# One core's hybrid SSD and retention layer: SSD output projection in block products, later norm transposes, first inputs by another queue

## The chip, the cores and the metric

The kernel runs on one core of one Trainium2 chip, as one program. The metric is device time in microseconds (us): the median of three runs.

## The reference

One decoder layer on 512 tokens of width 1024, all in float32. The stages that matter here, in order:

```
proj = x @ w_in                        # z, x|B|C, dt, q, k, v, g
y_ssd = norm(ssd_scan(...) * silu(z)) * norm_w      # 512 x 1024
y_ret = silu(g) * groupnorm(retention(q, k, v))     # 512 x 1024
mix = concat([y_ssd, y_ret]) @ w_mix_out            # (512 x 2048) @ (2048 x 1024)
x = LN(alpha * x + mix)
x = LN(alpha * x + cross_attention(x, mem))         # km = mem @ w_k, vm = mem @ w_v
h = conv3(x @ w_up + b_up); a, u = split(h)         # 2 x 2752 columns
x = LN(alpha * x + (silu(a) * u) @ w_down)
```

## The kernel before

**Products in three matmuls.** Each float32 operand is split into a high part (`wh`, a rounded copy made by ScalarE) and a low part (`wl`, the difference, made by VectorE or, for a few groups, by POOL). A product is the sum of high x high, high x low and low x high, three matmuls with up to 512 columns (`mm3`).

**Weights come in a planned stream.** `W` holds a list of weight groups of 128 x 1024 in the order of use. SP loads a group to a raw buffer (3 of them, tag `raw`), ScalarE and VectorE split it into a pair `wh`, `wl` (a ring of 4 pairs). `W.get` hands out the next pair and starts the split of the third one after it, which can run once the pair four before is no longer read. Groups made with `pool=True` (the eight for the memory keys) have their low part made by POOL.

**Block products.** `seven` multiplies a 512-token, 1024-row operand by a 1024 x 1024 matrix with seven products of halves instead of eight. The left operand's four blocks and their sums are made by a `Sides` object (`ready` makes the four sums for a piece, `make` splits a block), the weights' quarters and their sums by `Quarters` (eight loads of 128 x 1024, then `sums` on VectorE, L184 to L191, and splits, L196 and L197). Each product takes 2 weight pairs of 12 matmuls, goes to two PSUM banks, and its two results are added into the accumulator `acc` as they are done (`acc_quarter`). Without `seven`, `tok` does the same by 8 groups of 24 matmuls. The tuple `SEVEN` says which of four projections use it; before, these are the value projection `v` and the two halves of `down`. The SSD output projection has the branch in its code, which is not taken.

**The order around the SSD projection.** Before it come the last part of the z projection and then the output projection of the retention half (8 groups of 24 matmuls). Woven into this, TensorE transposes the finished SSD tiles (`ssd_out`: token tiles 0 to 3, eight 128 x 128 transposes each). Then comes the SSD half. As each of the four token tiles of `acc` is done, `norm(0, t)` runs: statistics on VectorE, a reciprocal root in two tiny POOL operations, two VectorE passes over 1024 columns (L957 and L964 before, six lines later after). TensorE goes on with the memory keys (8 groups with 256 columns, `keys`), then the memory values. `first_norm` sets after how many steps of these (a quarter of a key group, 0.68 us) the transposes of a normed tile come (`norm_t`).

**The MLP.** `up` is a stream of 43 groups of 24 matmuls. The first `down` block products are mixed into it: `UP_MIX` gives the number of up groups after each of the seven products, in the stream of weights and in TensorE's order alike.

**The start.** The input is transposed in four pieces of 256 rows. For the first, weights and input are loaded and split in halves; the rest goes by whole tiles of 512 KB. All these loads are issued by SP.

The order of instructions on each engine comes from a scheduler that follows the program's order and its own estimates; the engines run their lists in order.

Of the kernel before, what the change touches and what calls it, by code (L numbers as in the profile page):

```python
# [16 lines left out]
NT = 4  # L17
# [14 lines left out]
RAW = 3  # L32
NS = 37

SEVEN = ('v', 'down')
V_MIX = (1, 1, 1, 1, 0, 0, 0)
RET_MIX = (1, 1, 1, 1, 0, 0, 0)
UP_MIX = ((2, 2, 2, 2, 2, 2, 2), (1, 1, 1, 1, 1, 1, 1))

AHEAD = 4  # L40

# [18 lines left out]
def tile_layer(ctx, tc, wst, wdt, xt, xn, memt, rows, small_row, par, cst, mdec, out):  # L60
    nc = tc.nc
# [21 lines left out]
    def big(shape, dt=F32):  # L83
        return act.tile(shape, dt, tag="s", name=nm("s"), bufs=NS)
# [8 lines left out]
    def f(t):  # L93
        return t.bitcast(F32)
# [20 lines left out]
    def pair():  # L115
        return (ring.tile([P, 1024], F32R, tag="wh", name=nm("wh")),
                ring.tile([P, 1024], F32R, tag="wl", name=nm("wl")))

    def raw_slot():
        return ring.tile([P, 1024], F32, tag="raw", name=nm("raw"), bufs=RAW)  # L120

    class Group:
# [13 lines left out]
        def split(self, parts=1, between=None):  # L136
            r = raw_slot()
            h, l = pair()
            for i in range(parts):
                c = slice(i * 1024 // parts, (i + 1) * 1024 // parts)  # L140
                nc.sync.dma_start(out=r[:, c], in_=wst[self.n][:, c])
                copy = nc.vector.tensor_copy if parts > 1 and i == 0 else nc.scalar.copy
                copy(out=h[:, c], in_=r[:, c])  # L143
                (gtt if self.pool else tt)(out=l[:, c], in0=r[:, c], in1=f(h[:, c]), op=sub)  # L144
                if between is not None:
                    between(i, copy)
            return h, l
# [75 lines left out]
    def groups(n, k, pool=False):  # L223
        return [Group(n + i, pool) for i in range(k)]

    def mixed(products, others, after):

        out, others = [], list(others)
        for p, n in zip(products, after):
            out += p  # L230
            out += others[:n]
            others = others[n:]
        return out + others

    plan = groups(0, 8)
    plan += mixed(Quarters(8).items(), groups(16, 4), V_MIX) + groups(20, 8) if "v" in SEVEN else groups(8, 20)
    plan += groups(28, 12)
    plan += mixed(Quarters(44).items(), groups(40, 4), RET_MIX) if "ret" in SEVEN else groups(40, 12)
    plan += [q for p in Quarters(52, 8, 3).items() for q in p] if "ssd" in SEVEN else groups(52, 8)
    plan += groups(60, 8, True) + groups(68, 24)  # L240
    plan += groups(92, 4, True)
    up, down = groups(96, 12) + groups(116, 16) + groups(140, 11), groups(151, 6)
    if "down" in SEVEN:
        plan += up[:14] + mixed(Quarters(108).items(), up[14:28], UP_MIX[0])
        plan += up[28:30] + mixed(Quarters(132).items(), up[30:37], UP_MIX[1]) + up[37:]
    else:
        plan += up[:12] + groups(108, 8) + up[12:28] + groups(132, 8) + up[28:]
    plan += down
    W = Stream(plan)
# [75 lines left out]
    def behind(products, others, after):  # L325
        for p, n in zip(products, after):
            yield from p
            for _ in range(n):
                yield from next(others)
# [65 lines left out]
    def drain(*gens):  # L395
        for g in gens:
            for _ in g:
                pass
# [22 lines left out]
    for j in range(4):  # L421
        rv = big([P, 2, T])
        xv = xt[j].rearrange("p (k t) -> p k t", k=2)
        h, l = xT[j]
        x_raw.append(rv)

        def load_x(i, copy=nc.scalar.copy, n=1):
            nc.sync.dma_start(out=rv[:, i:i + n], in_=xv[:, i:i + n])
            copy(out=h[:, i:i + n], in_=rv[:, i:i + n])
            tt(out=l[:, i:i + n], in0=rv[:, i:i + n], in1=f(h[:, i:i + n]), op=sub)  # L430

        if j == 0:
            W.push(2, load_x)
        else:
            load_x(0, n=2)
            W.push()
# [142 lines left out]
    def x_quarter(i, j):  # L579
        return lambda k, t: x_lhs(4 * j + k, 2 * i + t)  # L580
# [22 lines left out]
    def k_and_v():  # L603
        if "v" in SEVEN:
            x_side = Sides(x_raw, {"11": x_quarter(0, 0), "12": x_quarter(0, 1), "22": x_quarter(1, 1)})
            for p in range(4):
                x_side.ready(p)
        yield from tok(x_lhs, all8, NT, rotary(1))
        if "v" in SEVEN:
            yield from behind(seven(x_side, v_quarter), bc_tiles(), V_MIX)  # L610
        else:
            for n in range(2):
                yield from tok(x_lhs, all8, NT, v_done(n))
# [382 lines left out]
    for j in range(2):  # L996
# [3 lines left out]
        rv = r.rearrange("p (k m) -> p k m", k=4)  # L1000
# [34 lines left out]
    xT = new_x()  # L1035

    def first_norm():
        for t in range(NT):
            yield 8
            norm_t(t)  # L1040

    dense = seq(keys(), *[tok(m_lhs, all8, 2, v_mem(n)) for n in range(2)])
# [186 lines left out]
    if "down" in SEVEN:  # L1229
        drain(*islice(up, 14))  # L1230
        drain(behind(seven(hid_side[0], acc_quarter(ALPHA)), up, UP_MIX[0]))
        drain(*islice(up, 2))
        drain(behind(seven(hid_side[1], acc_quarter()), up, UP_MIX[1]))
        drain(*up)
# [9 lines left out]
    for t in range(NT):  # L1244
        parts = THIRDS if t == NT - 1 else HALVES
# [141 lines left out]
```

## Time and profile before

| | |
|---|---|
| median of three runs | 928.28 us (928.28 to 928.32) |
| profiled execution | 928.88 us, of which its span is 926.4 us |
| TensorE matmuls | 911.5 us busy, 98% of the span |
| VectorE | 648.4 us, 70% |
| ScalarE | 369.6 us, 40% |
| POOL | 147.2 us, 16% |
| granted TensorE clock | 0.997 of 2.4 GHz |

The span runs from the first to the last instruction. The busy time of matmuls is modelled, since they overlap: one lasts 0.39 us in the rows while the next begins after 0.23. So waits are read from the starts.

### The profile page before, as it was taken

To read this page: it belongs to the slowest core of one execution; us is meant where nothing else is said; L and a number is where in the kernel's file an instruction comes from. 1 tells how busy PE (TensorE), PEld (TensorE's weight loads), DVE (VectorE), ACT (ScalarE), POOL (GpSimd) and SP (SyncE) were. 2 spreads that over 40 slices of the span, in tenths; PEclk is the share of its full clock that TensorE was granted. 3 is DMA by queue.
4 is the path that set the end of the run, shared out by engine and by line. 5 is a ranking of instruction groups with operands and counts; after the bars stand their busy time and mean duration, and the time that the engine had idled before them with its cause. 6 is when DMAs were issued, how large, how long until landed. Compare 5 with 4: busy or idle time off the path is not lost.

```text
span 926.4 us, 11580 instructions
## 1 busy us (share of the span) xinstructions
PE 911.5 (98%) x4535; PEld 757.0 (82%) x4535; DVE 648.4 (70%) x963; ACT 369.6 (40%) x545; POOL 147.2 (16%) x151
## 2 busy tenths in 40 slices
PE   9999999999999999999999999999999999999996
PEld 6788888877778888898888888988887888888885
DVE  5889757897854453478545669666779776897578
ACT  4236534355434431325434413543344443445330
POOL 1332011032525510163000007000000000000003
PEclk9999999999999999999999999999999999999998
DMA  7343122222212263426521222423333223331302
GB/s 287 105 146 127 39 76 69 69 69 70 69 46 69 91 230 109 138 92 205 190 82 46 69 69 95 134 91 98 108 133 118 68 69 114 125 119 52 114 23 91
DMA packets 26981, 95.24 MB, mean 103 GB/s; under 512 B 3120, under 2 KB 3632, under 8 KB 26928
## 3 DMA queue, kind: packets, MB, share of 16 engines
q1 hardware_dynamic: 25056, 88.09, 28.3%
q0 software_dynamic: 1728, 6.29, 2.0%
q8 instruction: 35, 0.57, 0.3%
q14 instruction: 18, 0.15, 0.0%
q10 hardware_dynamic: 144, 0.13, 0.0%
HBM read 92.41 MB, written 2.10 MB: 102 GB/s over the span
## 4 chain that ended last, share of the span: by engine, by line
PE 90%; DVE 5%; issue 1%; POOL 1%; DMA 1%; ACT 1%; SPq 0%; POOLq 0%; DVEq 0%
PE b L108 88%; PE b L112 3%; DVE s L964 1%; DMA s<-in_xt 1%; DVE s L957 1%; DVE st L952 1%; POOL st L465 1%; DVE s L1138 0%; DVE s L261 0%; DVE s L893 0%; DVE wl L197 0%; POOL st L464 0%; POOL s L960 0%; DVE wl L144 0%; DVE t L1175 0%
## 5 line engine op out<-in xcount | busy, mean ns | idle before, releaser
L108 PE MATMUL b<-s,wh 128*128 128x512 f32 (+1 forms) x1328 | 382.0, 372 | 3.3 <-DVE s L261 3.3
L108 PE MATMUL b<-wh,s 128*128 128x512 f32 (+1 forms) x1144 | 361.8, 391 | 0.6 <-DVE s L430 0.5
L108 PEld LDWEIGHTS b<-s,wh 128*128 128x128 f32 x1328 | 238.8, 189 | 47.2 <-DVE s L261 4.1
L108 PEld LDWEIGHTS b<-wh,s 128*128 128x128 f32 x1144 | 214.3, 188 | 48.3 <-DVE s L430 1.6
L144 DVE TENSOR_TENSOR wl<-raw,wh 128x1024 fp32r<-128x1024 f32 (+1 forms) x122 | 151.8, 1247 | 133.6 <-ACT wh L143 132.7
L108 PE MATMUL b<-s,wl 128*128 128x512 f32 (+1 forms) x664 | 245.1, 369 | 0.0
L143 ACT CAST wh<-raw 128x1024 fp32r<-128x1024 f32 (+1 forms) x133 | 139.2, 1049 | 215.8 <-PE b L108 195.1
L108 PE MATMUL b<-wl,s 128*128 128x512 f32 (+1 forms) x572 | 222.1, 388 | 1.4 <-DVE wl L197 1.4
L108 PEld LDWEIGHTS b<-s,wl 128*128 128x128 f32 x664 | 125.1, 188 | 21.3
L108 PEld LDWEIGHTS b<-wl,s 128*128 128x128 f32 x572 | 107.6, 188 | 23.6 <-DVE wl L197 1.7
L1175 DVE SCALAR_TENSOR_TENSOR t<-b,pr,t 128x511 f32<-128x511 f32 x86 | 64.2, 747 | 7.4 <-ACT t L1173 6.3
L197 DVE TENSOR_TENSOR wl<-s,wh 128x1024 fp32r<-128x1024 f32 x36 | 44.7, 1252 | 19.6 <-ACT wh L196 19.6
L196 ACT CAST wh<-s 128x1024 fp32r<-128x1024 f32 x36 | 37.8, 1053 | 50.2 <-PE b L108 40.7
L260 ACT CAST s<-b 128x512 fp32r<-128x512 f32 (+1 forms) x64 | 29.1, 484 | 55.7 <-PE b L112 22.5
L1201 POOL MEMSET t<- 64x512 f32 x1 | 0.5, 520 | 312.4 <-ACT t L1185 312.4
L144 POOL TENSOR_TENSOR wl<-raw,wh 128x1024 fp32r<-128x1024 f32 x12 | 32.7, 2738 | 68.2 <-ACT wh L143 68.2
L261 DVE TENSOR_TENSOR s<-b,s 128x512 fp32r<-128x512 f32 (+1 forms) x64 | 33.4, 550 | 13.9 <-ACT s L260 13.7
L1173 ACT ACTIVATE t<-b,cw,pr 128x512 f32<-128x512 f32 x43 | 33.3, 774 | 22.3 <-PE b L108 22.3
L893 DVE TENSOR_TENSOR s<-s,b 128x512 f32<-128x512 f32 x36 | 23.7, 680 | 15.4 <-PE b L108 15.4
L464 POOL TENSOR_TENSOR st<-st,epst 128x1 f32<-128x1 f32 (+1 forms) x16 | 5.6, 348 | 158.2 <-DVE st L953 157.8
L108 PEld LDWEIGHTS b<-s,t 128*128 128x128 f32 (+1 forms) x240 | 26.8, 180 | 3.1 <-PE b L108 0.9
L351 ACT CAST s<-s 128x512 fp32r<-128x512 f32 x36 | 20.7, 617 | 17.6 <-DVE s L1194 17.6
(164 smaller groups left out, 797.7 us busy)
## 6 DMA issues: line engine op xcount, KB each, us to landing
raw<-in_wst SPq DMA_DIRECT2D x132, 512.0 KB, 3.4
s<-in_wst SPq DMA_DIRECT2D x24, 512.0 KB, 4.7
s<-in_rows POOLq DMA_DIRECT2D x7, 512.0 KB, 6.2
s<-in_xn POOLq DMA_DIRECT2D x4, 512.0 KB, 5.8
s<-in_xt SPq DMA_DIRECT2D x3, 512.0 KB, 7.5
out_y<-s SPq DMA_DIRECT2D x3, 512.0 KB, 2.6
raw<-in_memt SPq DMA_DIRECT2D x2, 512.0 KB, 3.5
raw<-in_wst SPq DMA_DIRECT2D x2, 256.0 KB, 3.7
```

The lines of the kernel that those rows point to most:

```text
L108: pin(nc.tensor.matmul(o, lhsT=lhsT, rhs=rhs, start=start, stop=stop, skip_group_check=more))
L112: pin(nc.tensor.transpose(o, i, ident[:p, :p]))
L143: copy(out=h[:, c], in_=r[:, c])
L144: (gtt if self.pool else tt)(out=l[:, c], in0=r[:, c], in1=f(h[:, c]), op=sub)
L196: nc.scalar.copy(out=h, in_=src)
L197: tt(out=l, in0=src, in1=f(h), op=sub)
L260: nc.scalar.copy(out=h, in_=src)
L261: tt(out=l, in0=src, in1=f(h), op=sub)
L351: nc.scalar.copy(out=h[:, c, :], in_=src)
L893: tt(out=a, in0=a, in1=b, op=add)
L1173: nc.scalar.activation(out=c, in_=u, func=AF.Identity, bias=cw[0][:, i:i + 1], scale=ffp[:, i, 2:3])
L1175: stt(out=c[:, d:], in0=u[:, :T - d], scalar=ffp[:, i, 2 - d:3 - d], in1=c[:, d:], op0=mult, op1=add)
```

## The change

Five edits. The SSD output projection takes the branch with seven block products, and its weights are loaded as eight quarters (issued up to 8 groups ahead of the ring, summed up to 3 ahead). One up group moves from behind the last to behind the second down product. The first half of the input is issued from ScalarE's queue. The second input piece and second weights are loaded and split in halves, all by ScalarE and VectorE as for later ones. The transposes of the first normed tiles come after 13, 10, 10 and 8 steps instead of 8 each.

```diff
-SEVEN = ('v', 'down')
+SEVEN = ('v', 'ssd', 'down')
...
-UP_MIX = ((2, 2, 2, 2, 2, 2, 2), (1, 1, 1, 1, 1, 1, 1))
+UP_MIX = ((2, 3, 2, 2, 2, 2, 1), (1, 1, 1, 1, 1, 1, 1))
...
-                copy = nc.vector.tensor_copy if parts > 1 and i == 0 else nc.scalar.copy
+                copy = nc.vector.tensor_copy if between is not None and i == 0 else nc.scalar.copy
...
         def load_x(i, copy=nc.scalar.copy, n=1):
-            nc.sync.dma_start(out=rv[:, i:i + n], in_=xv[:, i:i + n])
+            if j > 0 or i > 0:
+                nc.sync.dma_start(out=rv[:, i:i + n], in_=xv[:, i:i + n])
             copy(out=h[:, i:i + n], in_=rv[:, i:i + n])
             tt(out=l[:, i:i + n], in0=rv[:, i:i + n], in1=f(h[:, i:i + n]), op=sub)

         if j == 0:
+            nc.scalar.dma_start(out=rv[:, 0:1], in_=xv[:, 0:1])
             W.push(2, load_x)
+        elif j == 1:
+            load_x(0)
+            W.push(2)
+            load_x(1)
         else:
...
     def first_norm():
-        for t in range(NT):
-            yield 8
+        for t, n in enumerate((13, 10, 10, 8)):
+            yield n
             norm_t(t)
```

VectorE before, at the end of the retention projection: the splits of plain weight groups and the four accumulations of its second half (L895).

```order
L144 TENSOR_TENSOR wl_2917<-raw_2915,wh_2916 128x1024
L144 TENSOR_TENSOR wl_2947<-raw_2945,wh_2946 128x1024
L144 TENSOR_TENSOR wl_2977<-raw_2975,wh_2976 128x1024
L895 SCALAR_TENSOR_TENSOR s_2681<-s_2681,b_2881 128x512
L895 SCALAR_TENSOR_TENSOR s_2682<-s_2682,b_2882 128x512
L895 SCALAR_TENSOR_TENSOR s_2683<-s_2683,b_2883 128x512
L895 SCALAR_TENSOR_TENSOR s_2684<-s_2684,b_2884 128x512
```

The same place after the change (L901 is the accumulation; 2908 and 2910 are the first quarters' two halves, 2912 is the second quarter's first half):

```order
L144 TENSOR_TENSOR wl_2926<-raw_2924,wh_2925 128x1024
L197 TENSOR_TENSOR wl_2955<-s_2908,wh_2954 128x1024
L184 TENSOR_TENSOR s_2908<-s_2916,s_2908 128x1024
L185 TENSOR_TENSOR s_2982<-s_2918,s_2908 128x1024
L197 TENSOR_TENSOR wl_2986<-s_2910,wh_2985 128x1024
L189 TENSOR_TENSOR s_2916<-s_2918,s_2916 128x1024
L184 TENSOR_TENSOR s_2910<-s_2920,s_2910 128x1024
L185 TENSOR_TENSOR s_3013<-s_2922,s_2910 128x1024
L189 TENSOR_TENSOR s_2920<-s_2922,s_2920 128x1024
L197 TENSOR_TENSOR wl_3017<-s_2912,wh_3016 128x1024
L901 SCALAR_TENSOR_TENSOR s_2687<-s_2687,b_2904 128x512
```

Six sums of weight quarters stand between the last weight splits and the last accumulations of the retention projection; the first of them needs the fifth of the eight loads.

POOL before, from the first key group on (L464 and L465 are a tile's reciprocal root):

```order
L144 TENSOR_TENSOR wl_3189<-raw_3187,wh_3188 128x1024
L144 TENSOR_TENSOR wl_3219<-raw_3217,wh_3218 128x1024
L144 TENSOR_TENSOR wl_3249<-raw_3247,wh_3248 128x1024
L464 TENSOR_TENSOR st_3262<-st_3261,epst 128x1
L465 TENSOR_TENSOR st_3262<-st_3262,mhalf 128x1
L464 TENSOR_TENSOR st_3279<-st_3278,epst 128x1
L465 TENSOR_TENSOR st_3279<-st_3279,mhalf 128x1
L144 TENSOR_TENSOR wl_3336<-raw_3334,wh_3335 128x1024
```

POOL after the change, the same place:

```order
L144 TENSOR_TENSOR wl_3292<-raw_3290,wh_3291 128x1024
L470 TENSOR_TENSOR st_3305<-st_3304,epst 128x1
L471 TENSOR_TENSOR st_3305<-st_3305,mhalf 128x1
L144 TENSOR_TENSOR wl_3332<-raw_3330,wh_3331 128x1024
L470 TENSOR_TENSOR st_3322<-st_3321,epst 128x1
L471 TENSOR_TENSOR st_3322<-st_3322,mhalf 128x1
L144 TENSOR_TENSOR wl_3350<-raw_3348,wh_3349 128x1024
L144 TENSOR_TENSOR wl_3403<-raw_3401,wh_3402 128x1024
```

The reciprocal roots of tiles 0 and 1 have moved ahead of the second and third key splits.

SP's first loads before the change (`raw` are weights, `s` the input):

```order
L141 DMA raw_94<-in_wst 128x512
L428 DMA s_93<-in_xt 128x512
L141 DMA raw_94<-in_wst 128x512
L428 DMA s_93<-in_xt 128x512
L141 DMA raw_113<-in_wst 128x1024
L428 DMA s_109<-in_xt 128x1024
L141 DMA raw_123<-in_wst 128x1024
```

And after it:

```order
L141 DMA raw_95<-in_wst 128x512 x2
L429 DMA s_93<-in_xt 128x512
L141 DMA raw_113<-in_wst 128x512 x2
L429 DMA s_109<-in_xt 128x512 x2
L141 DMA raw_129<-in_wst 128x1024
```

SP no longer issues the first half of the input, and the second weights and input have become two transfers each, the input's behind the weights'.

## Rows read from the trace of the kernel before

**Rows 1.** The page: TensorE's busy time, share of the span, instructions.

```profile
PE 911.5 (98%) x4535; PEld 757.0 (82%) x4535; DVE 648.4 (70%) x963; ACT 369.6 (40%) x545; POOL 147.2 (16%) x151
```

**Rows 2.** Chain of waits, 330 to 400: start, duration, what.

```profile
334.22 65.31 PE b L108 x288
```

**Rows 3.** VectorE's groups by shape: busy us, mean ns, idle before.

```profile
L197 DVE TENSOR_TENSOR wl<-s,wh 128x1024 fp32r<-128x1024 f32 x36 | 44.7, 1252 | 19.6 <-ACT wh L196 19.6
L352 DVE TENSOR_TENSOR s<-s,s 128x512 fp32r<-128x512 f32 x36 | 24.5, 703 | 2.2 <-ACT s L351 2.1
L893 DVE TENSOR_TENSOR s<-s,b 128x512 f32<-128x512 f32 x36 | 23.7, 680 | 15.4 <-PE b L108 15.4
...
L184 DVE TENSOR_TENSOR s<-s,s 128x1024 f32<-128x1024 f32 x6 | 7.3, 1223 | 0.1
```

**Rows 4.** VectorE's timeline, first down products: start, duration, count.

```profile
678.65 2.36 DVE L197 TENSOR_TENSOR wl<-s,wh 128x1024 fp32r<-128x1024 f32 x2
...
713.55 1.29 DVE L352 TENSOR_TENSOR s<-s,s 128x512 fp32r<-128x512 f32 x2
```

**Rows 5.** Stretches of two output projections: busy us of PE, PEld, DVE, ACT, POOL.

```profile
312.80:356.40 43.60, 43.60 (x210) 36.41 (x209) 20.72 (x26) 15.30 (x24) 11.41 (x21) 1.00 0.46 157
356.40:400.00 43.60, 43.60 (x194) 36.12 (x193) 15.59 (x19) 10.34 (x10) 5.45 (x3) 1.00 0.38 121
```

**Rows 6.** ScalarE's timeline: one of the casts, and its wait.

```profile
354.67 1.05 ACT L143 CAST wh<-raw 128x1024 fp32r<-128x1024 f32 x1 [4.38 <-PE b L108]
```

**Rows 7.** DMA issues: KB each, median us to landing.

```profile
s<-in_wst SPq DMA_DIRECT2D x24, 512.0 KB, 4.7
```

**Rows 8.** POOL's timeline, 388 to 426.

```profile
388.45 2.39 POOL L144 TENSOR_TENSOR wl<-raw,wh 128x1024 fp32r<-128x1024 f32 x1 [61.84 <-ACT wh L143]
...
402.07 0.56 POOL L465 TENSOR_TENSOR st<-st,mhalf 128x1 f32<-128x1 f32 x1
...
404.76 6.22 POOL L144 TENSOR_TENSOR wl<-raw,wh 128x1024 fp32r<-128x1024 f32 x2 [0.22 <-ACT wh L143]
...
420.42 5.72 POOL L144 TENSOR_TENSOR wl<-raw,wh 128x1024 fp32r<-128x1024 f32 x2
```

**Rows 9.** VectorE's timeline in the same stretch.

```profile
404.10 1.28 DVE L964 SCALAR_TENSOR_TENSOR s<-s,st,s 128x1024 f32<-128x1024 f32 x1
405.30 3.43 DVE L957 SCALAR_TENSOR_TENSOR s<-s,st,s 128x1024 f32<-128x1024 f32 x1
...
423.82 2.31 DVE L261 TENSOR_TENSOR s<-b,s 128x256 fp32r<-128x256 f32 x5
```

**Rows 10.** TensorE's timeline at the third set of transposes.

```profile
422.43 1.04 PE L112 MATMUL b<-cs,s 128*128 128x128 f32 x8
425.14 0.50 PE L108 MATMUL b<-s,wh 128*128 128x256 f32 x2 [1.68 <-DVE s L261]
```

**Rows 11.** TensorE's timeline in the third down product.

```profile
706.87 0.67 PE L108 MATMUL b<-wh,s 128*128 128x512 f32 x2
708.96 0.50 PE L108 MATMUL b<-wl,s 128*128 128x512 f32 x1 [1.41 <-DVE wl L197]
```

**Rows 12.** The start: SP, ScalarE, VectorE, TensorE in their timelines.

```profile
1.17 0.42 SPq L428 DMA_DIRECT2D s<-in_xt  x1
...
6.30 0.62 ACT L143 CAST wh<-raw 128x512 fp32r<-128x512 f32 x1 [4.29 <-DMA raw<-in_wst]
7.97 0.62 ACT L429 CAST s<-s 128x512 fp32r<-128x512 f32 x1 [1.05 <-DMA s<-in_xt]
9.32 1.05 ACT L143 CAST wh<-raw 128x1024 fp32r<-128x1024 f32 x1 [0.73 <-DMA raw<-in_wst]
10.56 1.06 ACT L429 CAST s<-s 128x1024 fp32r<-128x1024 f32 x1 [0.19 <-DMA s<-in_xt]
...
16.22 1.22 DVE L430 TENSOR_TENSOR s<-s,s 128x1024 fp32r<-128x1024 f32 x1
...
12.93 0.50 PE L108 MATMUL b<-wh,s 128*128 128x512 f32 x1 [0.51 <-DVE s L430]
```

## The prediction

> **What bounds the kernel now.** The page comes first [rows 1]: TensorE is busy for 98% of the span. So time is matmuls plus the few places where TensorE waits, and each edit is priced as matmuls removed plus waits removed, moved or made. The chain of waits gives the price of a matmul [rows 2]: 288 of them in 65.31 us, 0.2267 us each, across several changes of weights. Then I went through TensorE's timeline for starts further apart than that. From the output projections on there are three: in the memory keys at 423 us [rows 10], at the start of the MLP (the edit leaves it alone), and at 709 us inside the third block product of the first down projection [rows 11]. Others stand in the first 13 us [rows 12]. The tail behind the last matmul is untouched.
>
> **Part 1: 24 matmuls fewer.** The SSD projection goes from 2 x 8 x 4 x 3 = 192 matmuls to 7 x 2 x 2 x 2 x 3 = 168: 24 x 0.2267 = **-5.44 us**, if TensorE stays fed.
>
> *Is it fed?* VectorE gets most of the new work. By its durations [rows 3]: six more weight splits (14 pairs for 8) 6 x 1.25 = 7.5; eight sums of weight quarters, 8 x 1.22 = 9.8; eight sums of activation blocks of 512 columns, at the 0.70 of a split of that size, 5.6; 14 splits of these at 0.70, where there were 8 of transposes of the same size, 4.2; six more accumulations at 0.68, 4.1. Sum 31.2 us. The output projections of the two halves occupy 312.8 to 400, where VectorE is busy 20.7 and 15.6 us of 43.6 each [rows 5]. So 68 of some 82 us: possible if nothing stands late. VectorE is in order, so I follow its queue on the old time scale.
>
> The retention projection starts at 312.8; its eight weight pairs last 24 matmuls each (5.44), with four sets of transposes (0.87 each) between, so the SSD projection starts at S = 312.8 + 8 x 5.44 + 4 x 0.87 = 359.8, as now. Then a pair lasts 2.72, and E = S + 38.1 = 397.9 is its end. A pair is cast as soon as TensorE has left the pair four before: the casts start on that wait and take 1.05 [rows 6]. The eight quarter loads stand behind the two memory loads in SP's queue, and the second of these needs a raw buffer whose split can end at 334.1 (its ring place is left at 312.8 + 3 x 5.44 + 3 x 0.87 = 331.7; cast and split add 2.4). With 4.7 us for the first [rows 7] and 1.25 for each further one, the pace of whole loads in the first microseconds (9.32 to 10.56) [rows 12], all have landed by 349. VectorE's first sum of quarters can start at 345.8, behind the split of the first pair (343.5 + 2.3); the second pair's cast ends at 349.0 + 1.05. From there independent operations follow 1.14 us apart for 1024 columns and 0.60 for 512 (second starts inside 2.36 and 1.29 for two) [rows 4]. Counting on in the order shown: the fourth pair's low half is ready at 364.4, needed at S + 3 x 2.72 = 368.0; the sixth at 369.1, needed at 373.4; the last two at 386.7 and 389.3, needed at 392.5 and 395.2. Each product's accumulations end over 4 us before the next product but one takes their bank. I take **0** for this stage: a lead of 2.5 to 6 us covers it; without it each us is paid in full. Upper bound +4, with quarters landing 6 to 8 us later than I count.
>
> **Part 2: the memory keys and the later transposes.** The wait at 423 comes about so: the norm's last scalar-tensor-tensor stands against a POOL split of key weights (420.42 on) [rows 8], and lasts as long as the one begun at 405.30, 3.43 instead of 1.28 [rows 9]; behind it on VectorE stand the evictions that free the next PSUM bank (five from 423.82), and TensorE starts at 425.14 [rows 10]. Eight transposes take 0.87, so it lost 425.14 - 422.43 - 0.87 = 1.84 us. With the handover later (13, 10, 10, 8 steps) the evictions come before the bank is wanted.
>
> But another queue takes its place. POOL makes the low halves of the eight key pairs. Before, a pair of the projection lasted 24 matmuls, so POOL's first three splits ran before the norm, from 388.45 on. Now it lasts 12: the first can start at S + 11 x 2.72 + 1.05 = 390.8. POOL's order changes too, to one split and then the statistics of tile 0, where it was three. The rows show POOL's split and the norm's two long operations taking turns: alone 2.39 and 1.28 us, but the operation begun at 405.30 ends at 408.73, 1.09 after POOL's split (405.25 + 2.39), and POOL's second split ends at 404.76 + 6.22 = 410.98, 2.25 after that [rows 8, 9]. From 390.8 on: eight splits x 2.25 = 18.0; eight norm operations x 1.09 = 8.7; four reciprocal roots, each 0.56 for the power and about 0.2 for the sum, 3.0; about 0.9 of POOL waiting for a tile's statistics. Sum 421.4. TensorE wants the last at E + 7 x 2.72 + 2 x 0.87 = 418.7. That is 2.7 us of waiting for 1.84: **+0.9 us**. Bounds: -1.8 if POOL's splits go first throughout (390.8 + 18 + 3 = 411.8, in time), +4 if the evictions behind the norm hold a bank besides, as now.
>
> The Trainium skill's page "SBUF — State Buffer", section "Who interferes with whom", says that a VectorE instruction with two SBUF inputs and a GpSimd instruction that reads SBUF block each other entirely, whichever issues first. The rows of the norm agree (3.43 for 1.28). No row shows VectorE's weight split under a POOL split; by that rule the projection's last pair too would be held by up to 2.39, if VectorE came to it after 390.8. By my count it ends at 389.3.
>
> **Part 3: a third up group after the second down product.** The third product's second pair has its high weights at 706.87 (two matmuls, 0.45), and resumes with the low ones at 708.96 [rows 11]: 1.64 us lost to VectorE's split. The third group puts 5.44 us of matmuls ahead, so the low half is wanted 3 x 5.44 + 2.72 = 19.0 us after the second product's end. VectorE's list up to that split is nearly the same; its last wait is for the second group's bank (10.9 and 0.8 of ScalarE), then come two passes on that bank, two sums and the split, 4.9 us: 16.6 us, in time: **-1.64 us**. The group comes from behind the last product; the count before the next seven stays. Bounds 0 and -1.64.
>
> **Part 4: the first inputs.** ScalarE's casts start when a transfer lands: halves at 6.30 and 7.97, wholes at 9.32 and 10.56 [rows 12]. TensorE's matmul on the second input's low half waits until 12.93. An issue from ScalarE saves one of SP's, 0.42. Halving the second input and weights makes the last cast and split half as long (1.06 + 1.23 for the whole). Against this stand two more transfers, and here a half takes as long as a whole (1.67 between 6.30 and 7.97, 1.24 between 9.32 and 10.56). Gain bound: the third input's split ends at 17.44 as now, wanted at 12.93 + 24 x 0.2267 = 18.37: -0.9. Loss bound: two transfers x 1.24 later it ends at 19.9: +1.5. By bytes a half should cost half; the landings say more. I take a value between, **+0.3**.
>
> The skill's "DMA: Bandwidth & Descriptors", section "Issuing engines are not separate DMA queues", says that starting transfers on several engines saves the sequencer's issue time only. By it the first edit is worth at most that one issue.
>
> **Sum.** -5.44 + 0 + 0.9 - 1.64 + 0.3 = -5.9 us. The profiled execution took 928.88 (span 926.4), so 923.0; the runs' median, 928.28, is 0.6 lower: **922.4 us**.
>
> **Rivals.** *Keys without a wait* (POOL goes first, inputs gain 0.4): 928.28 - 5.44 - 1.84 - 1.64 - 0.4 = 919.0. For it: the handover now lies far behind the norm. Against: the turns in rows 8 and 9. Chance 0.20. *VectorE sets the pace in the projection*: about 3 us of waits from the third pair on, 925.4. For it the 68 of 82 us and the port rule; against it the lead counted above: 0.18. *All given back* (the same with the loss bounds of parts 2 and 4): 927 to 930: 0.08. *Slower*, by the quarter loads alone: they stand behind the memory loads, and VectorE stops at the first sum until its quarter lands, with all splits behind it. The last quarter is wanted at 353.7; beyond some 3.5 us of lead each us costs one. To end 1.9 us above the time before it must land near 365, sixteen after my count: 931. Against it, SP has nothing else to issue there: 0.06. My forecast, 921 to 925 by itself: 0.48.
>
> **Chances and range.** 0.2% (1.86 us) is about what a measurement can tell. Faster 0.86 (forecast 0.48, keys 0.20, VectorE 0.18), same 0.08, slower 0.06. The range 919.0 to 926.4 leaves out the lower half of the keys case and the last two.
>
> **What would show it.** Right: 168 matmuls in the projection at 0.2267 without a gap; POOL hardly idle from its first key split to its eighth, TensorE waiting on its low halves there; no wait in the third down product; the second input's matmuls under way between 12 and 13.5 us. Wrong: waits on quarter sums or weight splits in the projection; transposes waiting for their tile; the third input landing after 18 us.

## The result and the profile after

The changed kernel takes 924.01 us in the median of five runs (923.94 to 924.97); the kernel before, on the same chip, 928.32. The ratio is 0.995, with a 95% interval from 0.9937 to 0.9963: 4.3 us faster, where 5.9 were forecast. The sign and the range were right; two of the five terms of the sum were not, in opposite directions.

The profiled execution took 924.97 us, the slowest of the five; its span is 923.0 us, where the others have 922.1 to 922.2. The page's first part, to be held beside [rows 1]:

```profile
PE 908.1 (98%) x4511; PEld 755.4 (82%) x4511; DVE 680.0 (74%) x999; ACT 383.9 (42%) x575; POOL 149.4 (16%) x151
```

There are 24 matmuls fewer. 24 x 0.2267 is 5.44 us, but TensorE's busy time fell by 3.4 only. So either its matmuls got slower somewhere, or records hide a wait. Lines are six later than before. To find the place, I put the starts of the same matmuls of both traces side by side (behind the projection, the numbering is shifted by 24). The distance between them changes in four places and nowhere else:

| place | start before | start after | step |
|---|---|---|---|
| 60th matmul (counted from 0) | 18.73 | 17.48 | -1.25 |
| in the second key pair, behind the SSD projection | 407.15 | 400.45 | -5.45 |
| behind the keys | 453.89 | 451.86 | +4.67 |
| last matmul, behind the third down product | 918.35 | 914.55 | -1.77 |

The sum is -3.80. These are starts in one execution of each kernel, so a step holds to a few tenths of a us (how far for the first is shown with the two halves of the start edits). The last output lands 0.4 later in this one execution, so the span is 3.4 shorter.

**The projection.** The chain of waits after (start, duration, what), beside [rows 2], and VectorE's busy time (the third figure behind the length) in the same two stretches as [rows 5], the second cut off at the end of the projection:

```profile
332.97 55.79 PE b L108 x246
```

```profile
312.80:356.40 43.60, 43.60 (x210) 36.40 (x210) 29.56 (x35) 18.45 (x35) 10.40 (x18) 1.00 0.62 229
356.40:396.40 40.00, 40.00 (x178) 33.15 (x177) 39.22 (x51) 19.97 (x24) 6.35 (x5) 1.00 0.13 40
```

The reader is to see 55.79 / 246 = 0.2268 us per matmul, without a break, although VectorE is busy for 39.22 of 40.00 us in the second stretch. The last weight split, on VectorE:

```profile
387.19 1.23 DVE L197 TENSOR_TENSOR wl<-s,wh 128x1024 fp32r<-128x1024 f32 x1 [0.21 <-ACT wh L196]
```

It ends at 388.42. The forecast had 389.3 on the old time scale, 388.05 with the 1.25 us that the start gained.

**The memory keys.** TensorE's timeline after, where [rows 10] showed the wait before; in brackets the idle time and what ended it:

```profile
419.00 0.28 PE L108 MATMUL b<-s,wl 128*128 128x256 f32 x1
420.36 0.50 PE L108 MATMUL b<-s,wh 128*128 128x256 f32 x2 [1.07 <-ACT wh L143]
422.79 0.58 PE L108 MATMUL b<-s,wl 128*128 128x256 f32 x1 [1.93 <-POOL wl L144]
423.17 0.64 PE L108 MATMUL b<-s,wh 128*128 128x256 f32 x2
```

And the stretches of this stage (behind the length: busy time of PE, PEld, DVE, ACT, POOL, then the granted clock):

```profile
415.00:419.00 4.00, 3.88 (x33) 3.68 (x31) 3.52 (x4) 0.66 (x3) 1.35 (x1) 1.00 0.42 136
419.00:423.00 4.00, 0.99 (x6) 0.59 (x5) 2.35 (x3) 3.28 (x6) 2.62 (x2) 0.84 0.01 4
423.00:428.50 5.50, 5.50 (x24) 5.32 (x25) 4.87 (x8) 3.12 (x5) 0.81 (x2) 0.50 0.72 259
428.50:436.00 7.50, 7.50 (x38) 6.28 (x37) 3.56 (x7) 3.23 (x7) 0.00 (x0) 1.00 0.71 270
```

TensorE waits twice at the eighth key pair: first for ScalarE's cast, then for POOL's low half. From start to start these are 1.35 and 2.21 us where 0.12 is usual, so 3.3 us. And then the third row says "busy for 5.50 of 5.50" at a granted clock of 0.50, that is 1.2 GHz instead of 2.4: the matmuls begin 0.21 apart instead of 0.12. A busy share hides this; the clock column shows it. In the kernel before there was no such stretch.

This adds up to the step in the table. Held against one matmul each 0.12 us (256 columns) or 0.23 us (512), TensorE loses 3.3 us in the two waits, 2.7 in the slow stretch and 0.5 in three short waits just ahead; the bank wait of 1.84 is gone. 3.3 + 2.7 + 0.5 - 1.84 = 4.66.

What released each step is in the chain of waits after:

```profile
406.50 5.73 POOL wl L144 x2
412.24 1.13 POOL st L470
...
413.45 0.55 POOL st L471
...
414.03 3.40 DVE s L970
417.43 0.35 DVE s L261
...
417.80 0.38 ACT s L260
...
418.20 0.77 DVE s L261 x2
...
419.26 1.06 ACT wh L143
...
420.38 2.37 POOL wl L144
```

Read it upwards from the end. POOL's eighth split waits for ScalarE's cast of the eighth pair. This cast stands in ScalarE's list behind evictions (L260), these wait for VectorE's evictions (L261), these stand behind the second pass of the last tile's norm (L970), and this waits for the root (L471), which stands on POOL behind two key splits. POOL itself sat idle for 4.04 us ahead of its eighth split:

```profile
413.96 2.38 POOL L144 TENSOR_TENSOR wl<-raw,wh 128x1024 fp32r<-128x1024 f32 x1
420.38 2.36 POOL L144 TENSOR_TENSOR wl<-raw,wh 128x1024 fp32r<-128x1024 f32 x1 [4.04 <-ACT wh L143]
```

This trace also has a row of which the forecast found none, a weight split on VectorE beside a POOL split (the last one above). It takes 2.05 us, alone 1.22 (beside other work of POOL the kernel before has such a split of 2.59 us, at 205.72):

```profile
421.77 2.05 DVE L144 TENSOR_TENSOR wl<-raw,wh 128x1024 fp32r<-128x1024 f32 x1 [0.25 <-ACT wh L143]
```

**Start and third down product.** ScalarE's casts of the second input's second half and of the third input after, beside [rows 12]:

```profile
9.31 0.62 ACT L430 CAST s<-s 128x512 fp32r<-128x512 f32 x1 [0.19 <-DMA s<-in_xt]
...
13.14 1.05 ACT L430 CAST s<-s 128x1024 fp32r<-128x1024 f32 x1 [0.23 <-DMA s<-in_xt]
```

The third input is cast at 13.14, where the cast began at 15.13 before:

```profile
15.13 1.05 ACT L429 CAST s<-s 128x1024 fp32r<-128x1024 f32 x1 [0.17 <-DMA s<-in_xt]
```

No matmul of the second input waits. Of the wait at 709 us [rows 11] nothing is left. The chain of waits has one piece from the MLP's start to 898.4 us, where the last norms take over in the chain: 1464 matmuls, 0.218 us apart on average. The matmuls behind it, up to 914.55, have no gap either.

```profile
579.31 319.07 PE b L108 x1464
```

### The profile page after: what moved, and what is told of

It is laid out like the page before. It is cut to its first block, busy times and chain, and to the rows that moved or that the text cites. A ratio compares the mean times of both kernels' runs of the same rounds, so it can differ in the third digit from the quotient of the medians.

```text
span 923.0 us, 11614 instructions
## 1 busy us (share of the span) xinstructions
PE 908.1 (98%) x4511; PEld 755.4 (82%) x4511; DVE 680.0 (74%) x999; ACT 383.9 (42%) x575; POOL 149.4 (16%) x151
## 4 chain that ended last, share of the span: by engine, by line
PE 91%; POOL 3%; DVE 3%; issue 1%; ACT 1%; DMA 0%; POOLq 0%; DVEq 0%; ACTq 0%
PE b L108 88%; PE b L112 3%; POOL wl L144 2%; DVE s L970 1%; POOL st L470 1%; POOL st L471 1%; DVE st L958 1%; DMA raw<-in_wst 0%; DVE s L1144 0%; DVE s L261 0%; ACT wh L143 0%; DVE wl L144 0%; POOL s L966 0%; DVE s L963 0%; ACT s L965 0%
## 5 line engine op out<-in xcount | busy, mean ns | idle before, releaser
L108 PE MATMUL b<-wh,s 128*128 128x512 f32 (+1 forms) x1128 | 357.0, 391 | 0.1
L144 DVE TENSOR_TENSOR wl<-raw,wh 128x1024 fp32r<-128x1024 f32 (+1 forms) x115 | 142.9, 1245 | 109.1 <-ACT wh L143 108.6
L108 PE MATMUL b<-wl,s 128*128 128x512 f32 (+1 forms) x564 | 219.2, 389 | 0.0
L143 ACT CAST wh<-raw 128x1024 fp32r<-128x1024 f32 (+1 forms) x126 | 131.1, 1042 | 177.9 <-PE b L108 152.9
L196 ACT CAST wh<-s 128x1024 fp32r<-128x1024 f32 x50 | 52.5, 1053 | 77.9 <-PE b L108 59.7
L197 DVE TENSOR_TENSOR wl<-s,wh 128x1024 fp32r<-128x1024 f32 x50 | 61.6, 1242 | 21.8 <-ACT wh L196 21.8
L260 ACT CAST s<-b 128x256 fp32r<-128x256 f32 (+1 forms) x56 | 25.2, 464 | 55.7 <-DVE s L261 19.6
L261 DVE TENSOR_TENSOR s<-b,s 128x256 fp32r<-128x256 f32 (+1 forms) x56 | 28.8, 532 | 15.4 <-ACT s L260 15.0
L351 ACT CAST s<-s 128x512 fp32r<-128x512 f32 x50 | 28.8, 619 | 17.6 <-DVE s L1200 17.6
L352 DVE TENSOR_TENSOR s<-s,s 128x512 fp32r<-128x512 f32 x50 | 33.6, 696 | 3.0 <-ACT s L351 3.0
```

Of the source, the lines that this page charges most:

```text
L108: pin(nc.tensor.matmul(o, lhsT=lhsT, rhs=rhs, start=start, stop=stop, skip_group_check=more))
L196: nc.scalar.copy(out=h, in_=src)
L197: tt(out=l, in0=src, in1=f(h), op=sub)
L260: nc.scalar.copy(out=h, in_=src)
L261: tt(out=l, in0=src, in1=f(h), op=sub)
L351: nc.scalar.copy(out=h[:, c, :], in_=src)
```

## Experiments

The theory after the comparison: the loss is at the keys, made by POOL's splits and the norm in turn, by the cast that gets stuck behind them, and by the clock that falls behind the waits. The rivals: VectorE is simply too full there; the later handover is at fault; the clock falls for a reason of its own. First, the edits one at a time on the kernel before. "Last matmul" is the start of TensorE's last matmul in the profiled execution, 918.35 before.

**Start edits alone.**

```diff
-                copy = nc.vector.tensor_copy if parts > 1 and i == 0 else nc.scalar.copy
+                copy = nc.vector.tensor_copy if between is not None and i == 0 else nc.scalar.copy
...
-            nc.sync.dma_start(out=rv[:, i:i + n], in_=xv[:, i:i + n])
+            if j > 0 or i > 0:
+                nc.sync.dma_start(out=rv[:, i:i + n], in_=xv[:, i:i + n])
...
+            nc.scalar.dma_start(out=rv[:, 0:1], in_=xv[:, 0:1])
             W.push(2, load_x)
+        elif j == 1:
+            load_x(0)
+            W.push(2)
+            load_x(1)
```

> The kernel before with the edits of the start alone (first input half issued from ScalarE's queue; second input and second weights in halves). The forecast's term: +0.3 us, 928.6. Reading of the trace after: the wait before the second input's matmuls is gone for good and everything behind it starts 1.25 us earlier, 927.0. A third view, that the gain at the start is eaten later by loads that come late in the first projection: 928.3, no change.

Measured: 927.73 us (11 runs), before 928.38, ratio 0.9992 (0.9983 to 1.0001). The time alone decides little; the trace does. The 60th matmul starts at 17.48, and everything up to the MLP 1.27 us earlier than before. But the last matmul starts at 918.57, 0.2 later than before. The reason is the granted clock (seventh figure behind the length), here and below the value of the kernel before in the same stretch:

```profile
571.00:573.00 2.00, 2.00 (x11) 2.00 (x11) 1.90 (x4) 0.00 (x0) 2.00 (x2) 0.50 0.63 229
573.00:575.00 2.00, 2.00 (x15) 2.00 (x14) 2.00 (x1) 0.38 (x2) 2.00 (x2) 0.72 0.75 262
```

```profile
571.00:573.00 2.00, 1.72 (x15) 1.52 (x14) 1.97 (x5) 1.05 (x1) 2.00 (x1) 1.00 0.49 141
573.00:575.00 2.00, 2.00 (x19) 2.00 (x19) 1.93 (x3) 0.63 (x2) 2.00 (x2) 1.00 0.63 201
```

Both kernels have the same two waits at the MLP's start (1.65 and 0.56 us from start to start). Behind them the clock fell in one and not in the other, at a price of 1.5 us. Nine of the eleven runs lie at 927.6 to 927.9 and two, the profiled one among them, at 929.0 and 929.1; the mean granted clock is 0.997 to 0.998 in the nine and 0.996 in the two. That fits executions without and with this fall.

**Third up group alone.**

```diff
-UP_MIX = ((2, 2, 2, 2, 2, 2, 2), (1, 1, 1, 1, 1, 1, 1))
+UP_MIX = ((2, 3, 2, 2, 2, 2, 1), (1, 1, 1, 1, 1, 1, 1))
```

> The kernel before with the third up group behind the second down product alone. The forecast's term: -1.64 us, 926.6, with no wait left in the third down product. The trace after shows -1.77 there. The rival, that the wait moves to another product's bank or weights: 927.5 to 928.3 and a new gap between 700 and 800 us.

Measured: 926.31 (9 runs), before 928.38, ratio 0.9979 (0.9969 to 0.9989). The last matmul starts at 916.48, 1.87 earlier, 0.1 of it gained at the start; no gap is left behind 572 us. The term holds, and the wait did not move elsewhere.

**Later handover alone.**

```diff
-        for t in range(NT):
-            yield 8
+        for t, n in enumerate((13, 10, 10, 8)):
+            yield n
```

> The kernel before with the later handover of the first normed tiles alone (13, 10, 10, 8 steps). The forecast's step taken alone: the bank wait of 1.84 us goes and nothing replaces it while a pair of the projection still lasts 24 matmuls, 926.4. The rival: POOL's last two key splits (420.4 to 426.1 before) are then wanted earlier, pair 7 at 422.4 and pair 8 at 425.2, and TensorE waits about 1 us on them, 927.5.

Measured: 927.33 (11 runs), before 928.38, ratio 0.9988 (0.9979 to 0.9997). The wait for the bank is gone, and a shorter one for POOL has come at the eighth pair:

```profile
425.88 0.39 PE L108 MATMUL b<-s,wl 128*128 128x256 f32 x1 [0.43 <-POOL wl L144]
```

From start to start it is 0.71 instead of 0.12. So the edit gains 1.84 - 0.59 = 1.25 us of matmul starts and not 1.84: the rival was the nearer. (In the profiled execution the clock then fell at the MLP's start, as with the start edits.)

**Block products alone.**

```diff
-SEVEN = ('v', 'down')
+SEVEN = ('v', 'ssd', 'down')
```

> The kernel before with the block products of the SSD projection alone (handover still after 8 steps each). If only TensorE's matmuls count: -5.44 us, 922.8. The forecast's POOL and VectorE turns with the old bank wait kept: about -5.44 + 2.7, 925.6. Reading of the trace after (waits of 3.3 us at the eighth key pair and a stretch at half the granted clock behind them, together 6.5 us where there were 1.84): -5.44 + 4.66, 927.5, with the same stretch at a granted clock of 0.50.

Measured: 923.26 (5 runs), before 928.38, ratio 0.9951 (0.9938 to 0.9963). This edit by itself is worth as much as all five together. With the old handover TensorE waits for the bank at the third tile's transposes (2.21 us from start to start, 1.96 before), POOL's eighth split costs 0.25, and the clock stays at 1.00. My expectation of 927.5 took the loss of the changed kernel for one of the block products; it needs the later handover as well. The wait for the bank:

```profile
419.73 0.50 PE L108 MATMUL b<-s,wh 128*128 128x256 f32 x2 [1.94 <-DVE s L261]
```

Alone, the four edits gain 0.65 (start), 2.07, 1.05 and 5.12 us in the medians, 8.9 in sum; together they gain 4.3. So they act on each other, and the next runs ask where.

The next four change the changed kernel itself, whose last matmul starts at 914.55.

**Matmuls to fill the wait.** 27 matmuls more, on operands that lie ready.

```diff
             for j in range(2):
+                if h == XH - 1 and j == 1:
+                    for _ in range(FILL):
+                        mmul(b[:, 256:512], memk[0][0][:, 0, :P], memk[0][0][:, 0, :])
                 yield from feat(mk, 256, lambda o: None, b[:, j * 256:(j + 1) * 256])
```

> The changed kernel with 27 matmuls of 256 columns more on TensorE, just ahead of the eighth key pair (into the half bank that the pair's first matmuls start afresh, so the result is the same). They fill 3.06 of the 3.34 us that TensorE waits there. Theory A, the granted clock fell to 0.50 because TensorE stood idle, and the 24 to 27 matmuls behind the wait lost about 2.8 us by that: 921.3, with a clock of 1.00 behind the eighth pair. Rival B, the clock falls for another reason or the wait lengthens by the filler: 924.0 or more.

Measured: 923.11 (5 runs), before 929.8 on that chip, ratio 0.9934 (0.9921 to 0.9946). The ratios of these four kernels flatter them a little: of the nine runs of the kernel before on that chip, five have a mean granted clock of 0.996 and take 929.8 to 930.3 us, the other four 0.997 and 928.2 to 929.0. So the starts of the last matmul are the better measure. The stretches, to be held beside those of the changed kernel above:

```profile
419.00:423.00 4.00, 3.92 (x33) 3.72 (x32) 2.32 (x3) 3.30 (x6) 2.60 (x2) 1.00 0.01 4
423.00:428.50 5.50, 5.50 (x39) 5.11 (x40) 4.86 (x8) 3.13 (x5) 0.87 (x2) 1.00 0.83 250
```

POOL's eighth split is where it was (420.40), the cast too; only TensorE no longer stands idle, and the clock stays at 1.00. The last matmul starts at 912.39, 2.2 us earlier, with 27 matmuls more. One trace each would not be enough, since the clock does not fall in every execution (see the last section); but the mean granted clock is 0.995 or 0.996 in all five runs of the changed kernel and 0.997 or 0.998 in all five here. So the clock's fall was due to TensorE's idling. Undoing it gave back 2.2 us, somewhat less than theory A's 2.8; the filled kernel has 0.3 us of new short waits at 437 us.

**All key splits on VectorE.**

```diff
-    plan += groups(60, 8, True) + groups(68, 24)
+    plan += groups(60, 32)
```

> The changed kernel with the low halves of all eight key pairs made by VectorE instead of POOL. Theory A, the turns that POOL's splits and the norm's long operations take (3.4 us for 1.28, eight times) are what makes VectorE late: without them VectorE has about 30.4 us of work from 388.3 on, up to the eighth split, and ends near 418.7, wanted at 419.1: no or under 1 us of waiting, clock 1.00, 917.5 to 919. Rival B, VectorE is the bound of this stage whoever holds the port: ten us more work on it make TensorE wait longer, 925 to 930.

Measured: 922.06 (5 runs), before 929.8, ratio 0.9918 (0.9905 to 0.9932). Between the two theories. The turns are gone, each long pass of the norm takes 1.28 again, and there is no wait at the eighth pair. But the fourth pair's split, which POOL had begun at about 402, now stands behind the norm of the third tile, and TensorE waits for it. In the profiled execution it loses its clock behind this wait:

```profile
408.07 0.39 PE L108 MATMUL b<-s,wl 128*128 128x256 f32 x1 [2.19 <-DVE wl L144]
```

The stretch behind it:

```profile
409.00:413.00 4.00, 4.00 (x24) 4.00 (x23) 4.00 (x5) 1.42 (x2) 1.70 (x3) 0.57 0.72 214
```

**The last two key splits on VectorE.**

```diff
-    plan += groups(60, 8, True) + groups(68, 24)
+    plan += groups(60, 6, True) + groups(66, 26)
```

> The changed kernel with the low halves of the last two key pairs alone made by VectorE. Theory A: the norm of the last tile no longer takes turns with POOL, ends some 4 us earlier, the evictions behind it and with them ScalarE's cast of the eighth pair (419.26 in the changed kernel) come near 415.5, the split by 418: no wait, clock 1.00, 917.5. Rival B, the cast is late by its place behind the evictions in ScalarE's queue and not by the turns: the cast stays near 419, 921 to 924.

Measured: 919.66 (4 runs), before 929.8, ratio 0.9899 (0.9886 to 0.9913). The last matmul starts at 909.18, 5.4 earlier than in the changed kernel, at a clock of 1.00 in this stage. VectorE and ScalarE there:

```profile
414.23 1.28 DVE L970 SCALAR_TENSOR_TENSOR s<-s,st,s 128x1024 f32<-128x1024 f32 x1
415.43 1.22 DVE L144 TENSOR_TENSOR wl<-raw,wh 128x1024 fp32r<-128x1024 f32 x1
...
418.64 1.22 DVE L144 TENSOR_TENSOR wl<-raw,wh 128x1024 fp32r<-128x1024 f32 x1 [0.47 <-ACT wh L143]
```

```profile
417.55 1.06 ACT L143 CAST wh<-raw 128x1024 fp32r<-128x1024 f32 x1
```

The norm's last pass begins within 0.2 us of the same time as in the changed kernel (414.03), and takes 1.28 instead of 3.40, since POOL is idle beside it. The cast comes 1.7 us earlier, not 3.8 as theory A had it, for it still stands behind the evictions; but the split behind it takes VectorE 1.22 and not POOL 2.36. Together that is enough: the waits left at these two pairs are 0.37 and 0.25 us. VectorE has two splits more to make here and the stage is shorter all the same, so the rival "VectorE is simply too full there" is out.

**The early handover in the changed kernel.**

```diff
-        for t, n in enumerate((13, 10, 10, 8)):
-            yield n
+        for t in range(NT):
+            yield 8
```

> The changed kernel with the handover of the first normed tiles after 8 steps each again. The forecast's step: the bank wait of the kernel before (1.84 us) comes back, 925.9. Rival, POOL's last split and the cast ahead of it bound the stage whatever the handover: 924.0. A third way, the earlier evictions no longer stand behind the norm's last operations and the eighth cast comes sooner: 918 to 922.

Measured: 921.5 (4 runs), before 929.8, ratio 0.9917 (0.9903 to 0.993). The forecast's step, that the old handover is worse, is refuted in the changed kernel: the last matmul starts at 911.85, 2.7 us earlier. The bank wait is back:

```profile
418.93 0.50 PE L108 MATMUL b<-s,wh 128*128 128x256 f32 x2 [1.94 <-DVE s L261]
```

But it is one wait of 2.21 from start to start, and the time that it takes is what POOL's last split needed anyway: nothing is left to wait for at the eighth pair. The clock fell here as well, while the block products alone kept 1.00 behind the same wait of 2.21 us. The stretches of this kernel, then of the block products alone:

```profile
421.00:423.00 2.00, 2.00 (x11) 2.00 (x10) 1.86 (x4) 2.00 (x4) 2.00 (x3) 0.50 0.00 0
```

```profile
421.00:423.00 2.00, 2.00 (x18) 1.90 (x16) 1.99 (x5) 2.00 (x5) 2.00 (x1) 1.00 0.00 0
```

About half of the 2.7 us is the shorter slow stretch (some 15 matmuls at 0.50 here, some 25 in the changed kernel), the rest is waiting.

**The two halves of the start edits.** One kernel has only the issue from ScalarE's queue, the other only the halving of the second input and weights (and the `copy` line of the start edits, which goes with it).

```diff
-            nc.sync.dma_start(out=rv[:, i:i + n], in_=xv[:, i:i + n])
+            if j > 0 or i > 0:
+                nc.sync.dma_start(out=rv[:, i:i + n], in_=xv[:, i:i + n])
...
+            nc.scalar.dma_start(out=rv[:, 0:1], in_=xv[:, 0:1])
             W.push(2, load_x)
```

> The kernel before with the first half of the input issued from ScalarE's queue, and nothing else. If this edit is the gain at the start: TensorE's 60th matmul (18.73 us before, 17.48 after) comes near 17.5 and the wait at 12 us is gone. If it saves only SP's issue (0.42 us) it comes at 18.3 or later, with the wait before the second input still there.

```diff
             W.push(2, load_x)
+        elif j == 1:
+            load_x(0)
+            W.push(2)
+            load_x(1)
```

> The kernel before with the second input and the second weights loaded and split in halves, and nothing else. The forecast's step, a half lands no sooner than a whole: the wait at 12 us stays or grows and the 60th matmul comes at 18.7 to 20. The other reading, transfers in halves land one after the other and the work on the first half begins earlier: wait gone, 60th matmul near 17.5 to 17.9, with only the second half of the first input still late (0.2 to 0.6 us).

Measured: 927.49 and 927.51 (10 runs each), before 928.49, ratios 0.9992 (0.9983 to 1.0001) and 0.9991 (0.9982 to 1.0). The 60th matmul starts at 17.63 and at 17.59 (18.73 before, 17.48 with both): either edit alone removes the wait, and together they can't gain it twice. How much that is worth depends on the execution: the three other traces with the old start (third up group, later handover and block products alone) have the 60th matmul at 18.50 to 18.62, the eight with both edits at 17.48 to 17.92. So the gain is near 1.0, and the 1.25 of the pair above is at its upper end.

With the halves alone, ScalarE casts the two halves of the second weights and of the second input one behind the other, and waits for none of them:

```profile
8.30 1.30 ACT L143 CAST wh<-raw 128x512 fp32r<-128x512 f32 x2
9.65 1.28 ACT L429 CAST s<-s 128x512 fp32r<-128x512 f32 x2
```

With the issue alone, SP's queue at the third input's issue first, then ScalarE's casts of the second weights, the second input and the third input:

```profile
3.06 4.11 SPq L141 DMA_DIRECT2D raw<-in_wst  x2
7.22 0.43 SPq L429 DMA_DIRECT2D s<-in_xt  x1
```

```profile
8.22 1.05 ACT L143 CAST wh<-raw 128x1024 fp32r<-128x1024 f32 x1 [1.01 <-DMA raw<-in_wst]
9.48 1.06 ACT L430 CAST s<-s 128x1024 fp32r<-128x1024 f32 x1 [0.21 <-DMA s<-in_xt]
...
13.30 1.05 ACT L430 CAST s<-s 128x1024 fp32r<-128x1024 f32 x1 [0.22 <-DMA s<-in_xt]
```

These were at 9.32 and 10.56 [rows 12] and 15.13: 1.1 and 1.8 us earlier by an issue of 0.42. Part of that is scatter: the three other traces with the old start have them at 9.06 to 9.20, 10.32 to 10.46 and 14.23 to 14.40. Against these it is 0.8 to 1.1 us, still about twice the issue. SP's issue of the third input, at 7.22 here and at 8.04 before, does not account for this: in two of those three traces it stands at 7.16 and 7.22. From 3 to 5 us the transfers moved 309 GB/s, before 240 (stretches: the last two figures are the DMA engines' busy share and GB/s; the kernel with the issue, then the kernel before):

```profile
3.00:5.00 2.00, 2.00 (x6) 0.48 (x4) 0.75 (x3) 0.00 (x0) 0.00 (x0) 1.00 0.99 309
```

```profile
3.00:5.00 2.00, 2.00 (x6) 0.47 (x4) 1.41 (x3) 0.00 (x0) 0.00 (x0) 1.00 0.74 240
```

The three other traces with the old start have 244 to 271 GB/s there, the halves alone 265.

**Two more versions, at the MLP's start.** Both have the last two key splits on VectorE. The first also takes the first four up groups from POOL, the second the first two.

```diff
-    plan += groups(92, 4, True)
+    plan += groups(92, 4)
```

> The changed kernel with the last two key pairs and also the first four up groups of the MLP split by VectorE instead of POOL. If the turns between POOL's splits and the second norm (3.42 and 3.23 us for 1.28) make the two waits at the start of the MLP (1.53 and 0.44 us over the usual distance): both go, about 1.9 less than with the key pairs alone, 917.7. If VectorE's four splits (1.25 each) take the place of the turns: the same as with the key pairs alone, 919.7, or up to 3 us more with a wait on low halves there.

```diff
-    plan += groups(92, 4, True)
+    plan += groups(92, 2) + groups(94, 2, True)
```

> The changed kernel with the last two key pairs and the first two of the four up groups split by VectorE, the other two by POOL. If the first POOL split, which meets the norm's second pass, is what makes the wait, one such meeting remains or moves: 918 to 919.7. If the place of the splits in VectorE's queue matters more, 920 to 922.

Measured: 921.17 (5 runs), before 928.49, ratio 0.9922 (0.9909 to 0.9936), and 919.32 (4 runs), ratio 0.9905 (0.9892 to 0.9919). With all four on VectorE the wait there grows:

```profile
564.14 0.39 PE L108 MATMUL b<-s,wh 128*128 128x256 f32 x1 [2.44 <-DVE s L261]
```

It was 1.37 in this place, and with two on VectorE it is 1.31 (the version with the key splits alone, then this one):

```profile
562.88 0.39 PE L108 MATMUL b<-s,wh 128*128 128x256 f32 x1 [1.37 <-DVE s L261]
```

```profile
562.60 0.39 PE L108 MATMUL b<-s,wh 128*128 128x256 f32 x1 [1.31 <-DVE s L261]
```

The time with two can't be told from that of the version with the key splits alone. So taking the turns away does not shorten this wait: the norm's pass in turn with POOL held VectorE's evictions up for 3.3 us (557.82 to 561.16), and the pass with two splits in VectorE's own list holds them up for 3.5 (557.41 to 560.88). The guess was wrong, and 919.3 to 919.7 is the best that these runs reached.

## Why the prediction came out as it did

**The projection, -5.44 + 0: right** (-5.45). VectorE was as full as counted (29.6 + 39.2 = 68.8 us in the two stretches, 68 forecast), and the lead held: the last pair was ready 0.4 us from the time worked out by following its list, and over 5 us before TensorE wanted it. Counting busy time would have left it open; following the queue settled it.

**The third up group, -1.64: right** (-1.77, and -1.77 again when tried alone).

**The first inputs, +0.3: wrong in sign, -1.25 here and near -1.0 over all traces.** The step that failed is "a half takes as long as a whole", and with it the bound of one issue, 0.42, for the issue from ScalarE's queue. The two landings from which I took the first, 6.30 and 7.97, were not a rate of the transfers: ahead of them, from 3 to 5 us, the transfers moved less than later (240 GB/s, and 387 from 7 to 9), and with the halves alone four halves are cast from 8.30 to 10.93 with no wait for a transfer. The gain bound of -0.9 failed too: it kept the third input's split at 17.44, and with both edits that ends at 15.46. The Trainium skill's page "DMA: Bandwidth & Descriptors", section "Issuing engines are not separate DMA queues", says that a second issuing engine saves the sequencer's time only. Here, in the one trace of this edit alone, the casts came at least 0.8 us earlier than in any trace with the old start, for 0.42 of it, so the measurement goes beyond the page. How an issue of 0.42 comes to be worth that isn't shown.

**The memory keys, +0.9: the direction right, the size far off, +4.67.** The forecast said which resource would be late next (POOL's splits and the norm in turns, TensorE waiting on a low half) and had 2.7 us of waiting; 3.3 came. That these are so close is luck, for the chain is another one than the step counted, and both ends of the wait were off. By the turns, POOL was to need until 421.4 - 1.25 = 420.2 without a rest. It was done with seven splits at 416.3 and could have ended the eighth near 418.7: the step charged all eight norm passes a turn, and three of them ran in 1.27 to 1.55 us. TensorE was to come to the pair at 418.7 - 1.25 = 417.5 and came at 419.1: the step took 2.72 us for a key pair, as for a pair of the projection, but 24 matmuls 0.12 us apart are 2.87 (a quarter of a key group is 0.72 us and not 0.68), and short waits of 0.5 come on top. So POOL alone would have been in time. "POOL hardly idle", the forecast's own sign, is not what the trace shows. What held it was ScalarE's cast, behind evictions, behind the norm's last pass. The upper bound (+4, "if the evictions behind the norm hold a bank besides") names these evictions, and for another reason. That a POOL split and a norm pass take turns is seen again: 3.40 beside POOL, 1.28 without it. The Trainium skill's page "SBUF — State Buffer", section "Who interferes with whom", has the rule behind it, that a VectorE instruction with two SBUF inputs contends with a GpSimd (POOL) instruction that reads SBUF for a port that only one of them holds at a time. The trace agrees.

Two things were missing. First, the granted clock. I priced a wait as its length; behind these waits some 25 matmuls ran at 0.50, 2.7 us more than at 1.00, and filling the wait gave 2.2 us back. Second, the later handover was priced against the wait of the kernel before alone. There it gains 1.25; in the changed kernel it loses 2.7, since the bank wait had been covering the lateness of the eighth pair, and taking it away brought TensorE to that pair earlier, into two waits in place of one.

**Sum.** With the measured terms it is -1.25 - 5.45 + 4.67 - 1.77 = -3.8 in the profiled execution and -4.3 in the medians. The errors of the start (1.55 too high in this pair of executions) and of the keys (3.77 too low) partly cancelled. The likeliest case's own interval, 921 to 925, holds the result, but by luck more than by its working.

## What to carry to other kernels

A wait removed is worth its length only if the thing behind it is ready by then: before taking one away, ask what it has been covering, and follow the chain behind it over every engine's list, casts and evictions included, not only on the engine that looks busiest. Read the granted clock beside the busy share, for a busy stretch at 0.50 is a loss that no wait shows. And where two engines take turns on long operations, moving the last one or two pieces to the other engine can be worth more than the whole edit: here 5.4 us of matmul starts against the change's 3.8. Last, hold a small gain against several executions: the start's steps of 1.1 and 1.8 us between two traces were 0.8 to 1.1 against the others.

## What was not expected of the hardware

Waits of nearly the same length were followed by a fall of the clock in some executions and not in others. From start to start, and the lowest granted clock in the stretches behind:

| kernel | wait, us | clock behind it |
|---|---|---|
| before, keys | 1.96 | 1.00 |
| before, MLP's start | 1.65 and 0.56 | 1.00 |
| start edits alone, and later handover alone, MLP's start | 1.65 and 0.56 | 0.50 |
| block products alone, keys | 2.21 | 1.00 |
| changed, early handover, keys | 2.21 | 0.50 |
| all key splits on VectorE | 2.47 | 0.50 |
| changed kernel, keys | 1.35 and 2.21 | 0.50 |
| four up groups on VectorE, MLP's start | 2.72 and 0.56 | 1.00 |

The rows are one execution each, and the runs show that one and the same kernel has both: with the early handover two runs have a mean granted clock of 0.997 and 0.998 and take 920.76 and 920.85 us, two have 0.995 and take 922.15 and 922.32; with four up groups on VectorE two have 0.998 (920.48 and 920.62) and three 0.995 or 0.996 (921.17 to 921.74). Only the profiled ones show where the clock fell.

What decides between the two stays open; neither the length of the wait nor the kernel's order alone does. Where its cost could be read it was 1.5 us (start edits alone) and 2.2 us (filled wait), more than some of the edits are worth, and a median of four or five runs can move by as much with the number of falls in it.
